# Layer 0's banded attention and six more projection columns placed between the steps of the delta rule

## The chip, the core and the metric

One program runs on one core of a Trainium2 chip. The metric is the device time of one execution in microseconds (us). The core has five engines that each take their instructions in a fixed order and wait for each other by semaphores: TensorE (PE in the profile; PEld is its weight load), VectorE (DVE), ScalarE (ACT), GpSimd (POOL) and SyncE (SP), which here issues the loads of weights. Matrix products land in eight PSUM banks of 128 x 512 floats; all other tiles lie in SBUF.

## The reference, cut to what matters

256 context tokens and 256 latent tokens of width 1024 pass through two layers, then the latent tokens through a third one. All products are in float32. The change touches the mixer of layer 0 alone:

```python
def even_mixer(u_ctx, u_lat, w_in, w_out, a_prm, sink, rope_ang, need_ctx):
    p_ctx = u_ctx @ w_in
    p_lat = u_lat @ w_in
    a_lat, a_ctx = rwkv7_mixer(p_ctx[..., :A_IN], p_lat[..., :A_IN], a_prm, need_ctx)
    qc, kc, vc = split_qkv(p_ctx[..., A_IN:], B_HEADS, B_KV_HEADS)
    ql, kl, vl = split_qkv(p_lat[..., A_IN:], B_HEADS, B_KV_HEADS)
    ...
    b_lat = banded_window_attention(ql, kl, vl, kc, vc, sink_g)
    out_lat = jnp.concatenate([a_lat, b_lat], axis=-1) @ w_out
    ...
    b_ctx = context_attention(qc, kc, vc, sink_g)
    return out_lat, jnp.concatenate([a_ctx, b_ctx], axis=-1) @ w_out
```

The first half of the mixer's output comes from a recurrence over tokens (the delta rule, `rwkv7_scan`, 8 heads of 64, in both directions, first over the context and then over the latent tokens), the second half from attention of 8 heads in which a latent query sees its band and all context keys, and a context query the context. The two halves need nothing of each other until the product with `w_out`.

## The kernel before

The modulated activations of all 512 tokens lie transposed in `uh` and `ul`, two float32r parts whose sum is the float32 value; a weight tile is split in the same way (`wchunk`: ACT writes `whi`, DVE the rest into `wlo`), and each product takes three matmuls (L259 to L261). A column of the in-projection is 128 features: 24 matmuls of 512 tokens into a bank `psT`, and a token shift by `evac_a` (one ACT, two DVE instructions). Columns 0 to 11 are r, k, v of four pairs of heads t (columns t, 4 + t, 8 + t), columns 12 to 14 the low-rank inputs; k, v and q of the attention come first, in banks of their own.

Then `b_attn` (L734) attends four heads at a time (`attn4`, L661): scores `psS` in ring `B_S` of three banks, maximum, exponential, scaling `P`, transposes `psP` in ring `B_P` of two banks, the product with v in `psO` (bank 7), and the result as two float32r parts `moB`. A builder puts each engine's instructions in their final order ahead of time; it mixes this attention with the projection of 12 columns that stands behind it in the code (L779). Columns 3, 7, 11 follow at the delta rule's third step, after which `uh`, `ul` are given up and their room becomes a pool `rwb`.

The delta rule is 16 steps n = 4 t + 2 s + d (pair of heads t, sequence s, direction d). A step has three parts. `rwkv_par` (L827) prepares decay, keys and masked products (`pw`, `pa`, `gp`, `pbk`, `pkv`, with banks from ring `B_PREP`; POOL writes `kr` and `GA`), then forms `px` and inverts a triangular matrix in five rounds inside one bank of its own, `B_INV[n % 3]`. A round is: DVE transposes `TP` and ACT copies `SP` of the last `psx`, PE `pq`, DVE `Qm`, PE `psx`. The products `pwu` and `pqm` end it, and DVE and POOL make `QM` of `pqm`. `rwkv_rec` (L989) carries the state through four chunks: PE `yp<-S,QM`, then a copy of the state by ACT and DVE, four times in turn. What a step leaves for this lies in tiles numbered y = n % NY with NY = 4, and `KX` and `QM` of a step share one of them:

```python
        KX = tl([128, 2, 2, 128], "KX", f"KQ{y}")
        ...
        QM = tl([128, 4, 128], "QM", f"KQ{y}")
```

`KX` is written from `pkv` and `px` before the inversion starts (`px` stands in the same bank as the rounds), `QM` is last read by the step's last `yp<-S,QM`. Between the steps stand 12 chunks of the modulation for later layers (`ada_chunk`, `psA`, bank 7), the gates (`gates_out`), the group norm (`rwkv_out`) and `kappa`. The last step overlaps the product with `w_out` (`pso`, `proj0`).

Of the kernel before, what the change touches and what calls it, by code (L numbers as in the profile page):

```python
# [10 lines left out]
F32 = mybir.dt.float32  # L11
# [11 lines left out]
# ---------------------------------------------------------------- constants of the shapes  # L23


def _const_tables():
    """Arrays [128, n] that depend on shapes alone."""
# [24 lines left out]
    # rope tables, features on partitions, positions 0..255 on the free axis  # L52
# [43 lines left out]
    # columns of a row of the grid; query columns run backwards inside each half, flip puts them right  # L96
# [12 lines left out]
    # retention decay, [key j, head, i - j tile offset]  # L109
# [9 lines left out]
# groups of constants that are loaded together  # L119
# [16 lines left out]
# vectors laid out with features on partitions: name -> (offset, columns)  # L136
# [16 lines left out]
def body(ctx: ExitStack, tc: tile.TileContext, A, out, dbg=None):  # L153
# [9 lines left out]
    def ring(*banks):  # L163
        """takes the PSUM banks in turn"""
# [39 lines left out]
    def rsqrt(x, scale, eps, n, name):  # L204
        """(x * scale + eps) ** -0.5 for [128, n]"""
# [16 lines left out]
    mark = {}               # last instructions of a norm, by engine  # L222
    behind, free = [], [0]  # what the parts of the weights, but for the first ones, are queued behind
# [5 lines left out]
    def wchunk(W, r0, kt, c0, n):  # L229
        """rows r0 .. r0 + 128 kt, columns c0 .. c0 + n, as a sum of two float32r parts"""  # L230
# [18 lines left out]
    def wrows(W, r0, kt, c0, n=512):  # L249
        """list over the row tiles of (hi, lo) [128, n]"""  # L250
# [48 lines left out]
    # ------------------------------------------------------------ split of an activation  # L299
# [4 lines left out]
    # ------------------------------------------------------------ adaptive modulation  # L304
# [10 lines left out]
    def ada_chunk(l, j, pool=None, bank=None):  # L315
        """columns 512 j .. of layer l"""
# [705 lines left out]
    def gates_out(t, s=None):  # L1022
# [4 lines left out]
        if gwt[t] is None:  # L1027
            gwt[t] = rw.tile([128, 512], F32, name="gw", tag="gw")
# [48 lines left out]
    n = 0  # L1077
# [728 lines left out]
```

## Time and profile before

| what | value |
|---|---|
| time, median of 3 runs | 1856.71 us (1852.91 to 1860.09) |
| the profiled execution: span from first to last instruction | 1854.7 us |
| PE, DVE, ACT, POOL busy | 1756.5, 1113.8, 960.5, 462.2 us |
| first `pw` of the delta rule, first and last `pqm` | at 189.4, 261.7 and 537.2 us |

The profile shows one execution by its span; what lies around the span is not in it, so times of runs are compared with times of runs, and the span with spans. Busy time of PE counts a matmul up to its modelled end, so matmuls that follow each other overlap in it, and the distance from one start to the next is the better price of a matmul.

### The profile page before, as it was taken

What the parts mean: (1) busy time and instruction counts of PE and PEld (TensorE: products, weight loads), DVE (VectorE), ACT (ScalarE), POOL (GpSimd) and SP (SyncE); (2) the same over time, 40 slices, a digit from 0 to 9 for tenths busy, and PEclk for the clock granted to TensorE, in tenths of its full rate; (3) what the DMA queues carried; (4) which work ended last, traced back from release to release, by engine and by line L of the source; (5) the groups of instructions that cost most, each with busy time, mean ns of one, the idle gap of its engine ahead of it and who ended that gap; (6) DMA issues with size and microseconds to landing.
All of it is one profiled execution on the core that took longest, in us unless ns stands there. A gap on an engine that the chain in (4) does not pass through costs nothing.

```text
span 1854.7 us, 31823 instructions
## 1 busy us (share of the span) xinstructions
PE 1756.5 (95%) x12273; PEld 1453.3 (78%) x12273; DVE 1113.8 (60%) x2053; ACT 960.5 (52%) x1995; POOL 462.2 (25%) x566
## 2 busy tenths in 40 slices
PE   6999989998888999999999999899989999999998
PEld 4777557665666888888888876699978879989997
DVE  3676566777746425444456457545556787558676
ACT  4554367666745454434444545455545645446554
POOL 1220444544402253333334132111120122110000
PEclk9999899999989899999999989899999999999999
DMA  9311320222136345444432320356655725655553
GB/s 313 100 51 58 115 90 14 70 70 93 46 102 220 110 136 177 149 140 139 145 114 75 102 85 13 102 159 184 192 176 177 210 75 150 185 178 175 178 182 125
DMA packets 185399, 239.93 MB, mean 129 GB/s; under 512 B 8961, under 2 KB 127889, under 8 KB 185121
## 3 DMA queue, kind: packets, MB, share of 16 engines
q1 hardware_dynamic: 183056, 229.68, 40.0%
q0 software_dynamic: 1904, 7.70, 1.3%
q8 instruction: 97, 1.59, 0.4%
q14 instruction: 54, 0.43, 0.1%
q10 hardware_dynamic: 288, 0.52, 0.1%
HBM read 236.83 MB, written 1.05 MB: 128 GB/s over the span
## 4 chain that ended last, share of the span: by engine, by line
PE 79%; DVE 7%; ACT 5%; DMA 4%; issue 2%; POOL 2%; SPq 0%; POOLq 0%; DVEq 0%; ACTq 0%
PE psT L259 11%; PE psT L260 11%; PE psT L261 11%; PE pf L264 6%; PE pf L265 6%; PE pf L266 5%; PE psU L259 2%; PE psU L261 2%; PE psU L260 2%; PE psO L723 2%; PE psS L677 2%; DMA wada<-in_w_ada_dram 2%; PE psP L713 2%; PE psN L435 1%; ACT SP L947 1%
## 5 line engine op out<-in xcount | busy, mean ns | idle before, releaser
L245 DVE TENSOR_TENSOR wlo<-raw,whi 128x1024 fp32r<-128x1024 f32 x328 | 409.1, 1254 | 296.0 <-ACT whi L244 292.8
L244 ACT ACTIVATE whi<-raw 128x1024 fp32r<-128x1024 f32 x328 | 345.5, 1056 | 290.0 <-PE psT L260 142.7
L259 PE MATMUL psT<-uh,whi 128*128 128x256 f32 (+1 forms) x1200 | 385.6, 326 | 3.1 <-ACT uh L545 0.9
L260 PE MATMUL psT<-ul,whi 128*128 128x256 f32 (+1 forms) x1200 | 384.7, 322 | 0.0
L261 PE MATMUL psT<-uh,wlo 128*128 128x256 f32 (+1 forms) x1200 | 381.8, 321 | 0.0
L259 PEld LDWEIGHTS psT<-uh,whi 128*128 128x128 f32 x1200 | 226.5, 190 | 24.5 <-issue 2.2
L260 PEld LDWEIGHTS psT<-ul,whi 128*128 128x128 f32 x1200 | 227.1, 189 | 20.9 <-issue 2.3
L261 PEld LDWEIGHTS psT<-uh,wlo 128*128 128x128 f32 x1200 | 227.0, 189 | 17.8 <-issue 0.6
L266 PE MATMUL pf<-whi,hlo 128*128 128x512 f32 x472 | 182.4, 390 | 0.0
L265 PE MATMUL pf<-wlo,hh 128*128 128x512 f32 x472 | 182.3, 390 | 0.0
L264 PE MATMUL pf<-whi,hh 128*128 128x512 f32 x472 | 181.9, 392 | 0.0
L1149 POOL TENSOR_TENSOR ffr<-ffr 128x512 f32<-128x512 f32 (+1 forms) x64 | 61.3, 958 | 288.6 <-ACT hh L1148 257.2
L266 PEld LDWEIGHTS pf<-whi,hlo 128*128 128x128 f32 x472 | 88.6, 188 | 18.8 <-issue 0.2
L265 PEld LDWEIGHTS pf<-wlo,hh 128*128 128x128 f32 x472 | 88.7, 188 | 17.6
L264 PEld LDWEIGHTS pf<-whi,hh 128*128 128x128 f32 x472 | 88.5, 188 | 17.5
L259 PE MATMUL psU<-uh,whi 128*128 128x256 f32 x352 | 98.8, 282 | 1.0 <-DVE cv L1718 1.0
L261 PE MATMUL psU<-uh,wlo 128*128 128x256 f32 x352 | 98.3, 279 | 0.0
L260 PE MATMUL psU<-ul,whi 128*128 128x256 f32 x352 | 98.3, 279 | 0.0
L353 POOL TENSOR_TENSOR adac<-adac,wadc 128x512 f32<-128x512 f32 x56 | 77.9, 1391 | 64.7 <-ACT wadc L351 47.9
L1150 DVE TENSOR_TENSOR hlo<-ffr,hh 128x512 fp32r<-128x512 f32 (+1 forms) x64 | 46.5, 727 | 74.2 <-POOL ffr L1149 74.2
L351 ACT ACTIVATE wadc<-wadc,sT 128x512 f32<-128x512 f32 x56 | 40.5, 723 | 97.2 <-DMA wadc<-in_w_ada_dram 93.8
L947 ACT ACTIVATE SP<-psx 64x128 f32<-64x128 f32 x256 | 69.4, 271 | 36.8 <-DVE TP L945 32.0
(684 smaller groups left out, 3392.7 us busy)
## 6 DMA issues: line engine op xcount, KB each, us to landing
raw<-in_w_ff_dram SPq DMA_DIRECT2D x128, 512.0 KB, 4.2
wada<-in_w_ada_dram SPq DMA_DIRECT2D x64, 512.0 KB, 4.7
raw<-in_w_in_dram SPq DMA_DIRECT2D x50, 512.0 KB, 4.4
raw<-in_w_ffn_up_dram SPq DMA_DIRECT2D x44, 512.0 KB, 4.5
wadc<-in_w_ada_dram SPq DMA_DIRECT2D x64, 256.0 KB, 2.8
raw<-in_w_out_dram SPq DMA_DIRECT2D x24, 512.0 KB, 4.8
raw<-in_w_ffn_down_dram SPq DMA_DIRECT2D x22, 512.0 KB, 4.6
raw<-in_w_in_even_dram SPq DMA_DIRECT2D x21, 512.0 KB, 5.1
```

The lines of the kernel that those rows point to most:

```text
L244: S.activation(hi[:, :tot], raw[:, :tot], AF.Copy)
L245: V.tensor_tensor(lo[:, :tot], raw[:, :tot], R(hi[:, :tot]), op=OP.subtract)
L259: T.matmul(p_, wh, xh, start=first, stop=False)
L260: T.matmul(p_, wh, xl, start=False, stop=False)
L261: T.matmul(p_, wl, xh, start=False, stop=last)
L264: T.matmul(p_, xh, wh, start=first, stop=False)
L265: T.matmul(p_, xh, wl, start=False, stop=False)
L266: T.matmul(p_, xl, wh, start=False, stop=last)
L353: G.tensor_tensor(acc, acc, w, op=OP.add)
L947: S.activation(SP[HF[c], :, e, c, :], src[HF[e], :, c, :], AF.Copy)
L1149: G.tensor_tensor(r_, r_, r_, op=OP.mult)
L1150: V.tensor_tensor(hl_, r_, R(hh), op=OP.subtract)
```

## The change

`b_attn` goes. In its place `b_pair` treats two heads of one query tile (16 calls), and the loop over the steps calls it behind steps 2 to 13: first the eight pairs of the context, then the eight of the latent tokens. Its scores have bank 2 alone, its transposes and its output bank 7 alone, which `psA`, the gates and the group norm use too; `B_PREP` is left with banks 0 and 1. `P` and `PT` lie in the weights' tiles `whi` and `wlo`, and the result replaces the queries in `qB`, so that `moB` is not needed. For the latent pairs POOL scales both halves of `P` (before: one). Six columns of the projection stand ahead of the loop, three at its second step and six at its third (before: 12, none, 3). NY is 3, and tiles that had two buffers take one in `rw` and, in odd steps, one in `rwb`.

```diff
-    B_PREP, B_INV, B_REC = ring(0, 1, 2), (ring(3), ring(4), ring(5)), ring(6)
+    B_PREP, B_INV, B_REC = ring(0, 1), (ring(3), ring(4), ring(5)), ring(6)
+    B_AS, B_AP = ring(2), ring(7)
...
-    def b_attn():
...
+    def b_pair(seq, i, t):
+        q0, nk, g = seq * 256 + i * 128, 512 if seq else 256, t // 2
+        nt, one = nk // 128, nk == 256
+        ts_ = slice(q0, q0 + 128)
...
+        P = hl[0].tile([128, 1024], F32, name="P", tag="whi")[:, :2 * nk].rearrange("p (x k) -> p x k", x=2)
+        PT = hl[0].tile([128, 1024], F32, name="PT", tag="wlo")[:, :2 * nk].rearrange("p (x k) -> p x k", x=2)
+        sk = nsink[:, 2 * t:2 * t + 2]
+        for xs in ((0, 1),) if one else ((0,), (1,)):
+            p_ = B_AS("psS")
+            for x in xs:
+                for a in range(2):
+                    T.matmul(p_[:, (x * nk if one else 0):][:, :nk], qB[:, 2 * t + x, ts_], kB[a][:, g, :nk],
+                             start=a == 0 and not (one and x), stop=a == 1, skip_group_check=one)
+            if seq:
+                m_, o = (cst["bandA"], 384) if i == 0 else (cst["bandB"], 256)
+                V.tensor_tensor(p_[:, o:o + 128], p_[:, o:o + 128], m_, op=OP.add)
+            x_ = slice(xs[0], xs[-1] + 1)
+            V.tensor_reduce(nm[:, x_], p_.rearrange("p (x k) -> p x k", x=len(xs)), axis=AX.X, op=OP.max, negate=True)
+            V.tensor_tensor(nm[:, x_], nm[:, x_], sk[:, x_], op=OP.min)
+            for x in xs:
+                S.activation(P[:, x, :], p_[:, (x * nk if one else 0):][:, :nk], AF.Exp, bias=nm[:, x:x + 1],
+                             accum_out=sums[:, x:x + 1])
...
+        V.reciprocal(sums, sums)
+        for x in range(2):
+            (V if one else G).tensor_scalar(P[:, x, :], P[:, x, :], sums[:, x:x + 1], None, op0=OP.mult)
+        for xs in ((0, 1),) if one else ((0,), (1,)):
+            tr = B_AP("psP")
+            for n_, (x, j) in enumerate((x, j) for x in xs for j in range(nt)):
+                T.transpose(tr[:, n_ * 128:(n_ + 1) * 128], P[:, x, j * 128:(j + 1) * 128], ident)
+            d_ = PT[:, xs[0]:xs[-1] + 1, :].rearrange("p x k -> p (x k)")
+            if xs[0]:
+                V.tensor_copy(d_, tr)
+            else:
+                S.activation(d_, tr, AF.Copy)
+        o_ = B_AP("psO")
+        for j in range(nt):
+            for x in range(2):
+                T.matmul(o_[x * 64:x * 64 + 64, 0:128], vBn[:, j, g * 64:g * 64 + 64], PT[:, x, j * 128:(j + 1) * 128],
+                         start=j == 0, stop=j == nt - 1)
+        S.activation(qB[:, 2 * t, ts_], o_[:, 0:128], AF.Copy)
+        V.tensor_tensor(qB[:, 2 * t + 1, ts_], o_[:, 0:128], R(qB[:, 2 * t, ts_]), op=OP.subtract)
+    b_pairs = [(seq, i, t) for seq in (0, 1) for i in range(2) for t in range(4)]
...
-    NY, NZ = 4, 3
+    NY, NZ = 3, 3
...
-    b_attn()
-    proj_a((12, 13, 14) + tuple(x * 4 + t for t in range(3) for x in range(3)))
-    cpool(cm_at, cm_attB)
+    proj_a((12, 13, 14, 0, 4, 8))
...
-    late = {x + str(y) for x in ("kr", "GA", "Gt", "KQ", "RHS", "lam") for y in (2, 3)} | {"Qm2"}
+    late = {x + "2" for x in ("kr", "GA", "Gt", "KQ", "RHS", "lam", "Qm")}
...
+        odd = rb[0] is not None and n % 2 == 1
+        def tl(shape, name, tag, bufs=1):
+            pool = rb[0] if tag in late or (bufs == 2 and odd) else rw
+            return pool.tile(shape, F32, name=name, tag=tag, bufs=1)
...
+                if n == 1:
+                    proj_a((1, 5, 9), B_LATE)
                 if n == 2:
-                    proj_a((3, 7, 11), B_LATE)
+                    proj_a((2, 6, 10, 3, 7, 11), B_LATE)
...
                 n += 1
                 for a in later[len(later) * (n - 1) // 16:len(later) * n // 16]:
                     ada_chunk(*a)
+                for a in b_pairs[16 * max(n - 3, 0) // 12:16 * max(min(n - 2, 12), 0) // 12]:
+                    b_pair(*a)
```

PE's order in the middle of the delta rule. Before, around the `px` of step 8, the rows between the steps' products are those of `psA` alone:

```order
L840 MATMUL pw<-lora,W_747 128x256
L858 MATMUL pa<-lora,A_748 128x256
L1002 MATMUL yp<-S_0_753,QM 128x128
L958 MATMUL psx<-SP_769,Qm 64x128 x4
L336 MATMUL psA_3822<-cst_ci,adar 128x128 x4
L931 MATMUL px<-RHS,GK 64x64 x8
L331 MATMUL psA<-wada,sT 32x512 x4
L1002 MATMUL yp<-S_1_754,QM 128x128
```

Now, around the `px` of step 11, scores (`psS`), transposes (`psP`) and outputs (`psO`) of latent pairs stand between the same products:

```order
L882 MATMUL pw<-lora,W_739 128x256
L784 MATMUL psO<-PT,vBn 64x128 x8
L754 MATMUL psS<-kBh,qB 128x512
L754 MATMUL psS<-kBl,qB 128x512
L1000 MATMUL psx<-SP_763,Qm 64x128 x3
L1044 MATMUL yp<-S_3_748,QM 128x128
L1000 MATMUL psx<-SP_763,Qm 64x128
L973 MATMUL px<-RHS,GK 64x64 x8
L900 MATMUL pa<-lora,A_740 128x256
L775 MATMUL psP<-cst_ci,P 128x128 x4
L993 MATMUL pq<-TP_1833,GA 64x128 x4
L1044 MATMUL yp<-S_4_749,QM 128x128
```

All of the attention but its first four scores now stands behind the first `pw`, most of it between the steps' products as here; before, all of it stood ahead of the first `pw`.

ACT's order around `KX<-pkv` of step 6. Before, it and the `KX<-px` that follows stand ahead of the first state copy of step 3 (`COPY S_5`; step 3's other two, of `S_0` and `S_1`, come 8 and 15 rows later):

```order
L919 ACTIVATE KX<-pkv 128x4x64
L947 ACTIVATE SP_2477<-psx 64x2x64 x2
L920 ACTIVATE RHS<-pkv 64x4x64
L921 ACTIVATE RHS<-pkv 64x4x64
L947 ACTIVATE SP_769<-Sx 64x2x64 x4
L947 ACTIVATE SP_2477<-psx 64x2x64 x2
L947 ACTIVATE SP_771<-psx 64x2x64 x2
L842 ACTIVATE sg<-pw,hw_1830 128x256
L947 ACTIVATE SP_771<-psx 64x2x64 x2
L850 ACTIVATE E_3862<-cs 128x256
L932 ACTIVATE KX<-px 128x4x64
L1009 COPY S_5_758<-yp 64x64
```

Now the same `KX<-pkv` of step 6 stands behind all three state copies of step 3:

```order
L1051 COPY S_5_750<-yp 64x64
L989 ACTIVATE SP_1835<-psx 64x2x64 x2
L989 ACTIVATE SP_763<-psx 64x2x64 x2
L989 ACTIVATE SP_1835<-psx 64x2x64 x2
L1051 COPY S_0_745<-yp 64x64
L950 ACTIVATE Gt<-pbk 128x4x64 x2
L1051 COPY S_1_746<-yp 64x64
L1003 ACTIVATE SP_763<-psx 64x4x64 x2
L989 ACTIVATE SP_761<-Sx 64x2x64 x4
L989 ACTIVATE SP_1835<-psx 64x2x64 x2
L961 ACTIVATE KX<-pkv 128x4x64
L962 ACTIVATE RHS<-pkv 64x4x64
```

With NY = 3, `KX` of step n lies where `QM` of step n - 3 lay, and in the new order it follows the last read of that `QM` at every step from 3 on. On SP the 13 loads of 128-column weights stand as 7, four of `wada`, 6 (before 10, four, 3), and the 40 `wada` loads behind them in one row as before.

## Rows read from the trace of the kernel before

**Rows 1.** The page, span and part 1: busy us, share, instructions.

```profile
span 1854.7 us, 31823 instructions
PE 1756.5 (95%) x12273; PEld 1453.3 (78%) x12273; DVE 1113.8 (60%) x2053; ACT 960.5 (52%) x1995; POOL 462.2 (25%) x566
```

**Rows 2.** Busy us by stretch; columns in the first row.

```profile
core 0: us, PE busy (x) PEld busy (x) DVE busy (x) ACT busy (x) POOL busy (x), PEclk, DMA share, GB/s
66.00:189.00 123.00, 119.60 (x691) 93.64 (x689) 89.16 (x220) 63.40 (x146) 18.22 (x19) 0.97 0.23 68
189.00:262.00 73.00, 63.62 (x514) 41.85 (x510) 45.66 (x102) 37.51 (x103) 31.71 (x50) 0.93 0.36 109
262.00:535.00 273.00, 244.19 (x2919) 175.94 (x2914) 194.68 (x521) 181.82 (x586) 117.30 (x188) 0.95 0.17 55
...
408.00:432.00 24.00, 21.03 (x239) 15.04 (x237) 21.65 (x55) 14.86 (x49) 13.71 (x20) 0.93 0.03 4
...
535.00:620.00 85.00, 76.03 (x381) 57.62 (x378) 51.81 (x78) 44.78 (x80) 19.39 (x27) 0.88 0.66 222
```

**Rows 3.** Waits in 262 to 535 us: us in total, times, longest.

```profile
ACT SP L947 <- DVE TP L945: 28.6, 39, 2.3
```

**Rows 4.** Timeline of PE, start us, us, instruction, count: steps 0, 3, 12 and 15.

```profile
261.72 0.61 PE L977 MATMUL pqm<-Gt,TP 128*64 128x128 f32 x8
...
268.43 0.45 PE L931 MATMUL px<-RHS,GK 128*64 128x64 f32 x6
...
278.79 0.49 PE L1002 MATMUL yp<-S,QM 128*128 128x128 f32 x2
...
322.67 0.66 PE L977 MATMUL pqm<-Gt,TP 128*64 128x128 f32 x8
...
500.57 0.69 PE L931 MATMUL px<-RHS,GK 128*64 128x64 f32 x16 [0.15 <-PE psx L958]
...
506.37 0.38 PE L1002 MATMUL yp<-S,QM 128*128 128x128 f32 x2
...
537.24 0.61 PE L977 MATMUL pqm<-Gt,TP 128*64 128x128 f32 x8
```

**Rows 5.** Timeline of PE inside attention and projection.

```profile
119.17 0.40 PE L261 MATMUL psT<-uh,wlo 128*128 128x512 f32 x1
119.40 0.39 PE L259 MATMUL psT<-uh,whi 128*128 128x512 f32 x1
...
123.06 1.09 PE L723 MATMUL psO<-PT,vBn 128*64 128x128 f32 x14
124.07 1.09 PE L713 MATMUL psP<-cst_ci,P 128*128 128x128 f32 x8
124.92 0.48 PE L677 MATMUL psS<-kBh,qB 128*128 128x512 f32 x1
```

**Rows 6.** Timeline of PE at the attention's first score.

```profile
70.24 0.39 PE L261 MATMUL psT<-uh,wlo 128*128 128x512 f32 x1
74.03 0.80 PE L677 MATMUL psS<-kBh,qB 128*128 128x512 f32 x1 [3.40 <-DVE qB L599]
...
77.61 0.63 PE L260 MATMUL psT<-ul,whi 128*128 128x512 f32 x1
78.03 0.63 PE L261 MATMUL psT<-uh,wlo 128*128 128x512 f32 x1
```

**Rows 7.** Groups by line and form, 66 to 189 us: count, busy us, mean ns.

```profile
L704 POOL TENSOR_SCALAR P<-P,sums 128x512 f32<-128x512 f32 x8 | 14.7, 1837 | 58.0 <-DVE sums L702 50.3 <-PE psP L713 7.6
L688 DVE TENSOR_REDUCE nm<-psS 128x1 f32<-128x512 f32 x16 | 10.7, 681 | 0.1
L718 DVE COPY PT<-psP 128x512 f32<-128x512 f32 x8 | 5.5, 686 | 5.2 <-PE psP L713 5.1
L702 DVE RECIPROCAL sums<-sums 128x2 f32<-128x2 f32 x16 | 2.6, 160 | 0.2
```

**Rows 8.** Timeline of PE: one chunk of the modulation in bank 7.

```profile
352.44 1.06 PE L331 MATMUL psA<-wada,sT 128*32 128x512 f32 x8
...
362.05 0.66 PE L336 MATMUL psA<-cst_ci,adar 128*128 128x128 f32 x4
```

More of the change, by code (lines that the diff above doesn't have):

```diff
@@ L463, in close_all @@
         cpool(*opened[::-1])
-    cm_mob, mob = opool("mob", side="left")
+    cm_attB, attB = opool("attB", side="left")
     cm_hl, hl[0] = opool("hl0", bufs=2, side="left")
@@ L606, in stack_k, with tmpB @@
                 V.tensor_tensor(dl[HF[x], g, :], src[HF[g]], R(dh[HF[g], g, :]), op=OP.subtract)
+    tmps = [0]
+    def tmpB(name):
+        tmps[0] += 1
+        return mix.tile([128, 512], F32, name=name, tag=("kk", "yN", "bv")[tmps[0] % 3])
     def evac_b(tag, p_):
@@ L610, in evac_b @@
         if nm == "q":
-            q_ = attB.tile([128, 512], F32, name="qB_", tag="qB_", bufs=2)
+            q_ = tmpB("qB_")
             S.activation(q_, p_, AF.Copy, scale=0.125)
@@ L615, in evac_b @@
         elif nm == "k":
-            k_ = attB.tile([128, 512], F32, name="kB_", tag="qB_", bufs=2)
+            k_ = tmpB("kB_")
             S.activation(k_, p_, AF.Copy)
@@ L657, in body @@
     cm_rc, rc = opool("rwc", side="right")
-    cm_at, at = opool("at0", side="right")
     def attn4(pool, heads, qk, vf, nk, dst_h, dst_l, sink=None, bias=None, rq=None, flip=None):
@@ L727, in attn4 @@
         V.tensor_tensor(dst_l, ov, R(dst_h), op=OP.subtract)
-    moB = [mob.tile([128, 4, 512], F32R, name=n) for n in ("moBh", "moBl")]
     nsink = cp.tile([128, 8], F32, name="nsink")
@@ L732, in body @@
     V.tensor_scalar(nsink, nsink, -1.0, None, op0=OP.mult)
[L734 to L750 removed]
+    def b_pair(seq, i, t):
+        q0, nk, g = seq * 256 + i * 128, 512 if seq else 256, t // 2
+        nt, one = nk // 128, nk == 256
+        ts_ = slice(q0, q0 + 128)
+        nm = sm.tile([128, 2], F32, name="nm", tag="nm")
+        sums = sm.tile([128, 2], F32, name="sums", tag="sums")
+        P = hl[0].tile([128, 1024], F32, name="P", tag="whi")[:, :2 * nk].rearrange("p (x k) -> p x k", x=2)
[16 more added lines that the diff above has]
+                             accum_out=sums[:, x:x + 1])
+        es = sm.tile([128, 2], F32, name="es", tag="es")
+        V.tensor_tensor(es, nm, sk, op=OP.subtract)
+        S.activation(es, es, AF.Exp)
+        V.tensor_tensor(sums, sums, es, op=OP.add)
+        V.reciprocal(sums, sums)
[17 more added lines that the diff above has]
+        V.tensor_tensor(qB[:, 2 * t + 1, ts_], o_[:, 0:128], R(qB[:, 2 * t, ts_]), op=OP.subtract)
@@ L794, in body @@
     kkt, yNt, bvt = [None] * 4, [None] * 4, [None] * 4
+    rb = [None]
     def kappa(t):
-        kk = kkt[t] = mix.tile([128, 512], F32, name=f"kk{t}", tag="kk", bufs=2)
+        own = rb[0] if t % 2 else mix
+        kk = kkt[t] = own.tile([128, 512], F32, name=f"kk{t}", tag="kk")
         S.activation(kk, pT_of(4 + t), AF.Identity, scale=vec("a_k_k", t, 1))
@@ L816, in kappa @@
         V.tensor_tensor(kk, kk, p_, op=OP.mult)
-        yNt[t] = mix.tile([128, 4, 128], F32, name=f"yN{t}", tag="yN", bufs=2)
-        bvt[t] = mix.tile([128, 512], F32, name=f"bv{t}", tag="bv", bufs=2)
-    late = {x + str(y) for x in ("kr", "GA", "Gt", "KQ", "RHS", "lam") for y in (2, 3)} | {"Qm2"}
-    rb = [None]
+        yNt[t] = own.tile([128, 4, 128], F32, name=f"yN{t}", tag="yN")
+        bvt[t] = own.tile([128, 512], F32, name=f"bv{t}", tag="bv")
+    late = {x + "2" for x in ("kr", "GA", "Gt", "KQ", "RHS", "lam", "Qm")}
     hc = CDEC * 0.5
@@ L835, in rwkv_par @@
         tk = slice(256 * s, 256 * s + 256)
-        tl = lambda shape, name, tag, bufs=1: (rb[0] if tag in late else rw).tile(shape, F32, name=name, tag=tag,
-                                                                                  bufs=bufs)
+        odd = rb[0] is not None and n % 2 == 1
+        def tl(shape, name, tag, bufs=1):
+            pool = rb[0] if tag in late or (bufs == 2 and odd) else rw
+            return pool.tile(shape, F32, name=name, tag=tag, bufs=1)
         pw = pp("pw")[:, :256]
@@ L1027, in gates_out @@
         if gwt[t] is None:
-            gwt[t] = rw.tile([128, 512], F32, name="gw", tag="gw")
+            gwt[t] = rb[0].tile([128, 512], F32, name="gw", tag="gw")
         S.activation(gwt[t][:, tk], g_, AF.Identity, scale=vec("a_gn_w", t, 1))
@@ L1044, in rwkv_out @@
         V.tensor_tensor(y3, y3, mu[:, :2 * n, None].to_broadcast([128, 2 * n, 64]), op=OP.subtract)
-        sq = rw.tile([128, 512], F32, name="sqy", tag="sq")
+        sq = rb[0].tile([128, 512], F32, name="sqy", tag="sq")
         S.activation(sq[:, tk], yf, AF.Square)
@@ L1053, in rwkv_out @@
             T.transpose(p_[:, i * 128:(i + 1) * 128], y2[:, i, :], ident)
-        o_ = rw.tile([128, 512], F32, name="ya", tag="sq")
+        o_ = rb[0].tile([128, 512], F32, name="ya", tag="sq")
         V.tensor_tensor(o_[:, tk], p_[:, :128 * n], gwt[t][:, tk], op=OP.mult)
@@ L1071, in proj0 @@
                         f = 2 * (q % 2) + k
-                        x = [(moA[f][a] if q < 2 else moB[a][:, f, :])[:, i * 128:(i + 1) * 128] for a in range(2)]
+                        x = [(moA[f][a] if q < 2 else qB[:, 2 * f + a, :])[:, i * 128:(i + 1) * 128] for a in range(2)]
                         mmX(ps0[i, ch], *x, wh[:, k, :], wl[:, k, :], q == 2 and k == 0, q == 1 and k == 1)
@@ L1109, in body @@
     cpool(cm_rb, cm_rw, cm_rc)
-    if dbg == "mix0":
-        for t in range(8):
-            m_ = moA[t][0] if t < 4 else moB[0][:, t % 4, :]
-            nc.sync.dma_start(out[0, 128 * (t % 2):128 * (t % 2) + 128, (t // 2) * 256:(t // 2) * 256 + 256],
-                              R(m_[:, 256:512]))
-        close_all()
-        return
     cm_res, res = opool("res", side="right")
@@ L1182, in body @@
         after_mix0(i, [ps0[i, 0], ps0[i, 1]])
-    cpool(cm_mix, cm_hl, cm_mob)
+    cpool(cm_mix, cm_hl, cm_attB)
     cm_hl, hl1 = opool("hl1", bufs=4, side="left")
```

17 lines of the change are left out of this document (removed).

## The prediction

> **What bounds the kernel now.** The page gives PE 1756.5 of 1854.7 us, 95% [rows 1], but that share is an average over stages with different limits, so I read the busy time by stretch next [rows 2]. From 66 to 189 us, projection and attention, PE is busy 119.6 of 123 us and every other engine has room (DVE 89.2): here the time is what PE's instructions cost, and each one taken out gives its slot back. From 189 to 262, first `pw` to first `pqm`, PE idles 9.4 of 73 us. From 262 to 535, the steps, no engine is full (PE 89%, DVE 71%, ACT 67%, POOL 43%), and PE's weight load, 64%, shows that its 89% is partly matmuls that overlap. What binds there is a loop of latencies. The list of waits shows ACT waiting for DVE's `TP` 39 times, 28.6 us together [rows 3]: an inversion round goes DVE, ACT, PE, DVE, PE, and nothing shortens it.
>
> The timeline of PE gives that loop's size [rows 4]. Three inversions run at a time, in three banks. Step 3's `px` starts at 268.4, 6.7 us after step 0's first `pqm` (261.7), in the bank that this gives up, and its own last `pqm` ends at 323.3 (322.67 + 0.66): 54.9 us for an inversion. From step 3's `px` to step 15's, 500.57, four rounds of the three banks take 232 us, 58 us each; first to last `pqm` (261.7 to 537.2) is 275.5 us or five of them. One more fact matters for the change: step 3's `px` starts **10.9 us before** step 0's last `yp<-S,QM` ends (278.79 + 0.49), step 15's 6.2 us before step 12's ends (506.37 + 0.38); the mean over the 13 steps is 9.3. Today `KX` of step n and `QM` of step n - 3 lie in different tiles, so that overlap is free.
>
> **The change part by part.**
>
> *The front.* Attention's PE instructions leave a stretch that PE bounds. Slots are distances of starts [rows 5]: 14 `psO` take 1.01 us, 0.072 each, 8 `psP` 0.85, a 512-column matmul 0.23. 192 `psO` are 13.9 us, 96 `psP` 10.2, 32 latent scores 7.5, 32 context scores at half the columns 3.9 (estimate): 35.5. By the new order 16 context scores, four transposes and four pairs of outputs stay ahead of the first `pqm`, some 3 us. **−33.** The 504 matmuls of the r/k/v projection that stand ahead of the first `pqm` stay ahead of it in both orders (432 ahead of the first `pw` and 72 behind, now 358 and 146), so moving the columns saves nothing by count.
>
> *A stall and a slow clock.* The attention's first score waits 3.40 us for `qB`, and behind it 512-column matmuls start 0.42 us apart instead of 0.23 [rows 6], which costs 14 of them some 3 us. In the new order projection stands there. −6.4 if both go, 0 if the wait finds another place; most of it is the first score's own wait, so I take **−5**.
>
> *The room from 189 to 262.* 74 more projection matmuls (17 us at 0.23) stand behind the first `pw`, where PE idles 9.4 us. Between 0 and −9.4; part of that idle time is waits for loads, which stay: **−4**. So the first `pqm` comes 42 us earlier, at about 220.
>
> *The stretch of the steps.* This is the unknown. By the rows of the two orders DVE gets 61 us more between first and last `pqm`. Of the attention [rows 7]: 24 maxima at 0.68 (16.3), 8 copies at 0.69 (5.5), 72 small ones at 0.16 (11.5), and 48 masks, context scalings and result parts at an estimated 0.3 (15); together 48, of which 4 stand earlier. Then 12 for the preparation of one more step (a whole step is 194.7 / 15 = 13), 5 for four splits of weights. DVE's work becomes 194.7 + 61 = 256 us. Nothing lengthens if DVE may fill its idle 78 us: 0. At today's 71% busy it needs 360 us, +87; at the 90% of the densest slice, 408 to 432 [rows 2], 284, +11. PE gets 33 us of matmuls on 244.2 busy, but their slots are shorter than their busy times; POOL 16 scalings of 1.84, 29 us on 117, and a `GA` or `QM` queued behind one can be late by up to 1.84.
>
> The second price is a wait. With NY = 3 `KX` of step n takes the tile that `QM` of step n - 3 had. `KX<-pkv` on ACT must now wait for that step's last `yp<-S,QM`, and `px`, which stands in the inversion's bank, is copied behind it; queued behind that copy on ACT are the `SP` of the other two inversions, for which PE's `pq` wait. In the new order it already stands behind all the state copies, so it is not the semaphore but the order that spends the time. If inversion and recurrence take as long as today, each round of the three banks grows by the overlap lost, 9.3 us, and five rounds by 47. But with `px` later there is less competition: the last inversion, which has nothing behind it, took 37.3 us (500.57 to 537.85) against 54.9. I take a quarter of the 47 back: **+36**, which is also what DVE at 83% busy would give (256 / 0.83 = 308, +35). The two prices are not added, since a longer round is itself the room in which DVE does its 61 us; ends 0 and +61 (DVE's work all in series).
>
> The Trainium skill, "Perfetto Trace Analysis", section "Optimization Strategy", advises to interleave regimes whose most-contended engine differs. The rows agree that they differ (PE in the front, latencies in the steps); by that rule alone the attention would be hidden and the sum would be that of the first rival.
>
> *The tail.* 48 of the `pso` matmuls of the product with `w_out` now stand ahead of the last `pqm`, none before; at 0.23 that is 11 us. Behind the last `pqm` PE is busy 76 of 85 us, at a granted clock of 0.88, with 222 GB/s of loads [rows 2], so not all of it comes off: 0 to −11, taken **−6**.
>
> *At nothing:* the new buffers of one in `rw` (the tiles' writers in the new order follow their readers by a whole step), the result in `qB`, `P` in the weights' tiles (no weights are split in most of that stretch), the loads on SP (7, 4, 6 in place of 10, 4, 3, hidden behind matmuls of several us each; one late one costs a wait of a few us).
>
> **Sum:** −33 − 5 − 4 + 36 − 6 = −12; 1854.7 − 12 = 1842.7. The shown median lies 2.0 above the profile's span, so **1845 us**.
>
> **The rivals.**
>
> *Hidden.* The steps' idle time takes the attention; the stretch grows by under 25 us, about 12 (DVE at 90%). For it: DVE did run at 90% in one slice, and inversions may shorten as the last one did. Against it: a DVE so full delays every `TP` and `Qm`. 1854.7 − 42 − 6 + 12 + 2 = 1821 (1811 to 1833).
>
> *The hand-over paces (slower).* Mechanism: `KX` behind the state copies, 9.3 us per round, nothing taken back, and the fuller DVE and ACT lengthen an inversion by about 5 us (a fifth more instructions to stand behind on DVE). Five rounds of 14.3 are 71: 1854.7 − 48 + 71 + 2 = 1880. It decides as soon as a round grows by more than 9.6 us (48 for five). For it: both effects lie on the loop that binds. Against it: the last inversion's 37.3. The Trainium skill, same page and section, says that a gap which keeps coming back can mean that there is too little SBUF or PSUM for the next tile; NY = 3 would make such a gap, and by that rule the change ends here. No row of before can show it.
>
> *Bank 7 paces.* `psA`, transposes, outputs and gates take turns in it. One chunk of `psA` holds it from 352.4 to 362.7, 10.3 us [rows 8]; with 12 chunks over 16 steps that is 7.7 a step, and 1.33 pairs that hold it 5 to 10 us each add 7 to 13: 14 to 21 of the 18.4 us that a step takes. At 21 the stretch grows by 15 × 2.6 = 39, about as the forecast, some 42 with the gates: 1854.7 − 48 + 42 + 2 = 1851, no change. Against it: what a pair holds is only my estimate, and context pairs are half as long.
>
> **How the numbers follow.** A change of 0.5%, 9.3 us, is about what a measurement of this kernel can tell from none. Forecast (stretch +25 to +47, 1833 to 1856): 0.43, of which 0.28 faster by more than 0.5% and 0.15 within; hidden 0.25, all faster; hand-over 0.20, of which 0.17 slower and 0.03 within; bank 7 0.12, of which 0.09 within and 0.03 slower. Faster 0.53, same 0.27, slower 0.20. The range 1815 to 1872 leaves out the lower end of hidden (0.07) and the upper part of the hand-over (0.12). The likeliest case's own range is 1833 to 1856.
>
> **What would show it.** Right: first `pqm` near 220; first to last `pqm` about 311 us, DVE about 83% busy there; every `px` from step 3 on right behind the last `yp<-S,QM` of the step three before, where it now starts ahead of it; 79 instead of 85 us from there to the tail's end. Wrong: a first `pqm` later than 230 (then the front was not PE's alone); a round of three steps over 66 us (hand-over) or under 60 (hidden); PE waiting for bank 7 rather than for DVE and ACT between the steps.

## The result and the profile after

The changed kernel takes **1875.49 us** (median of 4 runs, 1871.74 to 1881.19) against 1857.14 before: ratio 1.0111, 95% interval 1.0087 to 1.0135. It is 1.1% slower, 3.5 us above the predicted range and on the other side of no change. The profiled execution spans 1869.9 us, 15.2 more than that of before. The page's part 1, beside [rows 1]:

```profile
PE 1756.4 (94%) x12273; PEld 1448.1 (77%) x12273; DVE 1113.6 (60%) x2049; ACT 961.8 (51%) x2007; POOL 474.0 (25%) x574
```

The work is the same, so the time is a matter of where it lies. The timeline of PE (start us, us, instruction, count), beside [rows 4]:

```profile
215.67 0.61 PE L1019 MATMUL pqm<-Gt,TP 128*64 128x128 f32 x8
...
233.65 0.49 PE L1044 MATMUL yp<-S,QM 128*128 128x128 f32 x2
...
241.06 0.64 PE L973 MATMUL px<-RHS,GK 128*64 128x64 f32 x16
...
285.90 0.61 PE L1019 MATMUL pqm<-Gt,TP 128*64 128x128 f32 x8
...
522.89 1.08 PE L973 MATMUL px<-RHS,GK 128*64 128x64 f32 x16
...
568.41 0.66 PE L1019 MATMUL pqm<-Gt,TP 128*64 128x128 f32 x8
```

The first `pqm` comes 46.0 us earlier (215.7 for 261.7). First to last `pqm` takes 352.7 us for 275.5: +77.2. From the last `pqm` to the end it is 1301.5 for 1317.5: −16.0. The three make +15.2. An inversion is shorter than before (step 3's 45.5 us for 54.9), but its `px` starts late: step 3's 241.06 stands 22 us behind the end of the inversion whose bank it takes, where before it stood 3.5 behind; the mean over steps 3 to 15 is 22.2 for 4.3. A round of three steps takes 70.5 us (281.83 / 4) for 58.0.

Busy time of the engines in exactly that stretch, before and then after (columns as in [rows 2]):

```profile
261.70:537.20 275.50, 246.35 (x2968) 177.60 (x2964) 195.89 (x525) 182.99 (x588) 117.60 (x188) 0.95 0.17 55
```

```profile
215.70:568.40 352.70, 308.36 (x3424) 218.95 (x3418) 247.11 (x675) 221.51 (x700) 149.65 (x214) 0.97 0.18 59
```

There are two differences. PE is busy 62.0 us longer, and it idles 44.3 us instead of 29.2. Summed over the timeline from each matmul's start to the next one's, idle time taken out, the attention's products take 38.5 of the 62 and the `pso` that came in from the tail 12.4; the other 11 are not accounted for here. The shares of the engines have hardly moved (PE 89% to 87%, DVE 71% to 70%): before, too, PE idled only 29 us in the whole stretch.

Half of the added idle time is one wait, that of the modulation's products `psA` for their loads `wada`: 12.5 us in 8 waits, before 4.9 in 5. Whether the stretch would be shorter without it was not tried.

### The profile page after: what moved, and what is told of

It is laid out like the page before. It is cut to its first block, busy times and chain, and to the rows that moved or that the text cites. A ratio compares the mean times of both kernels' runs of the same rounds, so it can differ in the third digit from the quotient of the medians.

```text
span 1869.9 us, 31775 instructions
## 1 busy us (share of the span) xinstructions
PE 1756.4 (94%) x12273; PEld 1448.1 (77%) x12273; DVE 1113.6 (60%) x2049; ACT 961.8 (51%) x2007; POOL 474.0 (25%) x574
## 4 chain that ended last, share of the span: by engine, by line
PE 75%; DVE 7%; DMA 6%; ACT 6%; issue 2%; POOL 2%; SPq 0%; POOLq 0%; ACTq 0%; DVEq 0%
PE psT L260 10%; PE psT L261 10%; PE psT L262 9%; PE pf L265 5%; PE pf L266 5%; PE pf L267 5%; DMA wada<-in_w_ada_dram 2%; PE psU L260 2%; PE psU L262 2%; PE psU L261 2%; DMA wadc<-in_w_ada_dram 2%; PE psA L332 1%; PE pso L266 1%; PE pso L265 1%; PE psN L436 1%
## 5 line engine op out<-in xcount | busy, mean ns | idle before, releaser
L266 PEld LDWEIGHTS pf<-wlo,hh 128*128 128x128 f32 x472 | 88.6, 188 | 18.3 <-DVE wlo L246 0.8
L989 ACT ACTIVATE SP<-psx 64x128 f32<-64x128 f32 x256 | 69.2, 270 | 44.3 <-DVE TP L987 38.2
```

Source lines behind the costliest of these rows:

```text
L266: T.matmul(p_, xh, wl, start=False, stop=False)
L989: S.activation(SP[HF[c], :, e, c, :], src[HF[e], :, c, :], AF.Copy)
```

## The experiments

All ratios are to the kernel before, measured in the same job; "stretch" is first to last `pqm` in the profile, the gap is the mean from the last `pqm` of step n - 3 to the `px` of step n.

| run | us | ratio, 95% interval | stretch | gap |
|---|---|---|---|---|
| before / changed kernel | 1857.14 / 1875.49 | 1.0111 (1.0087 to 1.0135) | 275.5 / 352.7 | 4.3 / 22.2 |
| 1: before, NY = 3 | 1883.76 | 1.0167 (1.0151 to 1.0184) | 318.3 | 15.7 |
| 2: before, two preparation banks | 1896.12 | 1.0234 (1.0217 to 1.0251) | 319.0 | 18.2 |
| 3: changed, NY = 4 | 1868.47 | 1.0089 (1.0072 to 1.0107) | 341.0 | 20.5 |
| 4: changed, no attention | 1856.63 | 1.0014 (1.0000 to 1.0027) | 333.3 | 18.5 |
| 5: changed, three banks, scores in bank 7 | 1931.04 | 1.0418 (1.0392 to 1.0443) | 329.1 | 16.3 |
| 6: as 5, NY = 4 | 1923.65 | 1.0361 (1.0337 to 1.0384) | 319.8 | 12.4 |
| 7: before, NY = 3 and two banks | 1910.13 | 1.0296 (1.0261 to 1.0331) | 340.5 | 19.2 |
| 8: changed, kappa in bank 2 | 1871.61 | 1.0104 (1.0086 to 1.0122) | 345.8 | 18.3 |
| 9: as 2, kappa in bank 2 | 1874.76 | 1.0114 (1.0069 to 1.0160) | 304.0 | 7.3 |
| 10: changed, ring of three with the scores | 1872.11 | 1.0118 (1.0084 to 1.0151) | 354.8 | 22.8 |
| 11: as 10, NY = 4 | 1856.51 | 1.0019 (1.0004 to 1.0034) | 339.5 | 17.2 |
| 12: as 8, NY = 4 | 1873.98 | 1.0084 (1.0059 to 1.0110) | 347.5 | 14.2 |
| 13: as 11, no attention | 1811.68 | 0.9762 (0.9738 to 0.9787) | 280.9 | 5.6 |
| 14: changed, half of the scalings on DVE | 1870.54 | 1.0073 (1.0051 to 1.0095) | 350.3 | 21.3 |
| 15: as 13, the pairs' DVE work alone | 1838.67 | 0.9901 (0.9885 to 0.9918) | 279.8 | 4.7 |
| 16: as 11, no row maxima | 1853.89 | 0.9995 (0.9975 to 1.0016) | 340.2 | 14.3 |
| 17: before, no row maxima | 1856.19 | 0.9991 (0.9981 to 1.0002) | 278.9 | 5.4 |
| 18: as 11, the pairs without DVE work | 1846.64 | 0.9967 (0.9955 to 0.9978) | 317.2 | 12.2 |

### The two layouts, alone in the kernel before

Run 1:

```diff
-    NY, NZ = 4, 3
+    NY, NZ = 3, 3
...
-    late = {x + str(y) for x in ("kr", "GA", "Gt", "KQ", "RHS", "lam") for y in (2, 3)} | {"Qm2"}
+    late = {x + "2" for x in ("kr", "GA", "Gt", "KQ", "RHS", "lam", "Qm")}
```

> The kernel before with NY = 3 (late tiles of the set 2 alone), nothing else: attention stays ahead of the steps, three banks for the preparation. Theory H (the hand-over of all tiles named by y: kr of step n is written over a tile that the QM of step n - 3 reads, so that the preparation from kr to px, some 17 us, can't start before the inversion n - 3 has ended): every kr from step 3 on begins behind the last pqm of step n - 3, a round of three steps grows from 58 to 68 to 75 us, first to last pqm from 275 to 320 to 350, time 1895 to 1925. Theory W (the attention's own work on the fuller engines and in bank 7 is what lengthens the stretch): no growth over 10 us, time 1855 to 1867. Theory P (two preparation banks): as W.

Run 2:

```diff
-    B_PREP, B_INV, B_REC = ring(0, 1, 2), ...
+    B_PREP, B_INV, B_REC = ring(0, 1), ...
```

> The kernel before with two banks (0 and 1) for the preparation instead of three, nothing else. Theory P (with gp holding both banks, pbk and pkv wait for the masked products, and that delays every px): first to last pqm 275 grows by 30 to 60, time 1885 to 1915. Theories H and W: the preparation has slack ahead of its inversion bank (kr stood 13 to 15 us ahead of the end of the inversion three steps before), growth under 10 us, time 1855 to 1867.

Both slow the kernel by more than the whole change does, with no attention in the steps: +31 us (theory H expected more, 1895 us at the least) and +44 us. In run 1 the preparation waits for the old tile. POOL's timeline in step 3 and its waits (us in total, times, longest) from 258 to 576 us:

```profile
262.31 0.73 POOL L868 TENSOR_TENSOR kr<-kk,sg 128x256 f32<-128x256 f32 x1 [2.29 <-DVE QM L978]
```

```profile
POOL RHS L923 <- PE yp L997: 28.8, 6, 14.5
...
POOL kr L868 <- DVE QM L978: 7.8, 6, 2.3
```

`kr` of step n lies on the `kr` that `QM` of step n - 3 reads, so it starts 1.5 us behind the end of that inversion on average, where before it started 12.3 us ahead of it, and `px` needs 14 us more from there. `RHS` lies in tiles numbered y too, and its memset on POOL waits for the old one's reader `yp<-RHS,Gt` (28.8 us in 6 waits, before 4.3 in one). The step's preparation is no longer hidden under the inversion.

The hand-over that ends last is still another one. In 11 of the 13 steps the last `yp<-S,QM` of step n - 3 ends 0.3 to 5.4 us behind the `pkv` of step n, and `KX<-pkv` follows both; `px` stands 3.0 us behind that `yp<-S,QM` on average. In step 3:

```profile
270.02 0.27 PE L915 MATMUL pkv<-cst_ci,rkv 128*128 128x128 f32 x1
...
274.15 0.49 PE L1002 MATMUL yp<-S,QM 128*128 128x128 f32 x2
```

```profile
275.14 0.39 ACT L919 ACTIVATE KX<-pkv 128x256 f32<-128x256 f32 x1
```

So with NY = 3 alone the wait for `KX` that the prediction named comes last. Without it `px` could come no more than some 4 us earlier (`KX<-pkv` stands 4.1 us behind `pkv` on average): the late `kr` comes right before it.

In run 2 the tiles are as before; the preparation itself is slower, and most of all where `kappa` stands between two steps. The same place in the changed kernel, PE's timeline behind step 6:

```profile
293.31 0.27 PE L957 MATMUL pkv<-cst_ci,rkv 128*128 128x128 f32 x1
294.76 1.05 PE L843 MATMUL ssp<-cst_c,sq 128*128 128x2 f32 x8
299.30 0.60 PE L850 MATMUL psr<-cst_ci,rsn 128*2 128x128 f32 x4
302.22 1.12 PE L854 MATMUL psr<-rnT,cst_c 2*128 2x512 f32 x2
303.27 0.70 PE L882 MATMUL pw<-lora,W 64*128 64x256 f32 x2
```

and in the kernel before:

```profile
319.09 0.27 PE L915 MATMUL pkv<-cst_ci,rkv 128*128 128x128 f32 x1
...
322.04 0.70 PE L840 MATMUL pw<-lora,W 64*128 64x256 f32 x2
```

With a third bank the next step's `pw` goes ahead beside `kappa` (2.95 us from the last `pkv`); with two, `kappa`'s three products hold the banks and `pw` follows the last of them (9.96 us). Three such places make 24 us more than before in the changed kernel and 21 more in run 2. The granted clock of the stretch was 0.91 in run 2 and 0.95 before, so at most some 15 of its 44 us can be the clock's (0.09 × 319 less 0.05 × 275.5, an estimate). Run 9 takes `kappa` out of the two banks of run 2:

```diff
+    B_KAP = ring(2)
...
-        ssp = B_PREP("ssp")
+        ssp = B_KAP("ssp")
...
-        p_ = B_PREP("psr")
+        p_ = B_KAP("psr")
```

> The kernel before with two preparation banks and kappa's products in bank 2, which is empty there. Theory K: about half of the 44 us that two banks cost alone comes back, time 1868 to 1882. Rival: time 1888 to 1898.

21 of the 44 us come back, as expected: `kappa` is half of the two banks' price. Run 7 has both layouts in the kernel before:

> The kernel before with both layouts of the change, NY = 3 and two preparation banks, attention and projection ahead as before. Theory M (the two losses are two ways for the same preparation to be late, and the longer one hides the other): stretch 318 to 330, time 1892 to 1908, near the run with two banks alone. Theory A (they add): stretch 355 to 365, time 1920 to 1935.

1910 lies between the theories (stretch 340.5): the two losses hide each other in part, 44 + 31 make 56 (1910.1 against 1854.45 in that job).

### The layouts undone in the changed kernel

Run 3 gives back NY = 4, run 4 leaves the attention out:

```diff
-    NY, NZ = 3, 3
+    NY, NZ = 4, 3
...
-            pool = rb[0] if tag in late or (bufs == 2 and odd) else rw
+            pool = rb[0] if tag in late or (bufs == 2 and odd and tag in ("cs", "bk", "GK")) else rw
```

```diff
-                    b_pair(*a)
+                    pass
```

> The changed kernel with NY = 4 again (tiles of sets 2 and 3 in the pool rwb); to make room, sg, E1, ic and b_ have one place each instead of two, cs, bk and GK keep two. Theory H: kr is written well ahead of the end of the inversion n - 3 again, px follows that end by about 5 us instead of 21, first to last pqm falls from 353 to 295 to 315, time 1820 to 1840. Theories W and P: the stretch stays at 340 to 355, time 1860 to 1880.

> The changed kernel with the 16 pairs of attention left out altogether (the second half of the mixer's output is then the queries), so that NY = 3, the two preparation banks and the moved columns stand alone. Theory H: the steps stay slow, first to last pqm 325 to 345 (353 with attention), px still 15 us or more behind the end of the inversion n - 3, time 1845 to 1865. Theory W: without the attention's work the stretch falls to the 275 us of before or below, time 1795 to 1815. Theory P: as H.

Runs 5 and 6 give back the third bank and put the scores into bank 7 (6 with run 3's edit too), run 8 puts `kappa` into bank 2 (`B_PREP` to `B_AS` in its three lines, as in run 9), run 12 adds NY = 4 to that, runs 10 and 11 let preparation and scores take three banks in turn (11 with NY = 4). The edits of 5 and of 10:

```diff
-    B_PREP, B_INV, B_REC = ring(0, 1), (ring(3), ring(4), ring(5)), ring(6)
-    B_AS, B_AP = ring(2), ring(7)
+    B_PREP, B_INV, B_REC = ring(0, 1, 2), (ring(3), ring(4), ring(5)), ring(6)
+    B_AS, B_AP = ring(7), ring(7)
```

```diff
-    B_PREP, B_INV, B_REC = ring(0, 1), (ring(3), ring(4), ring(5)), ring(6)
-    B_AS, B_AP = ring(2), ring(7)
+    B_PREP, B_INV, B_REC = ring(0, 1, 2), (ring(3), ring(4), ring(5)), ring(6)
+    B_AS, B_AP = B_PREP, ring(7)
```

> The changed kernel with three banks (0, 1, 2) for the preparation again; the attention's scores go to bank 7, to its transposes and outputs. NY stays 3. Theory P (in the changed kernel the serial preparation in two banks binds, 23.7 us from one pw to the next, and NY = 3 hides behind it): the preparation becomes faster until NY = 3 binds, as in the run of before with NY = 3 (62.6 us per three steps): stretch 353 falls to 325 to 340, time 1848 to 1865. Theory B7 (bank 7 is then the bound: scores, transposes, outputs, psA, gates in one bank): stretch 353 or longer, time 1872 to 1900.

> Both layouts of before in the changed kernel: three preparation banks (scores in bank 7) and NY = 4 (sg, E1, ic, b_ with one place). If the two layouts are all that lengthens the stretch beyond the attention's own 19 us: stretch 275 + 19 to 35 = 295 to 310, time 1810 to 1832, faster than both kernels. If bank 7 paces: stretch 340 or more, time 1860 and up.

> The changed kernel, with the three products of kappa (ssp, psr, psr) put into bank 2, where the attention's scores are, instead of the two preparation banks. Theory K (with two banks kappa, which stands between steps 2 and 3, 6 and 7, 10 and 11, holds the serial preparation: from pkv of those steps to the next pw 10 to 12 us, where before had 3): these three distances fall to 3 to 5 us, stretch 353 to 325 to 340, time 1850 to 1865. Rival (the two banks cost the same at every step, gp, pbk and pkv waiting for each other): the distances may fall but px does not come earlier, time 1868 to 1880.

> The changed kernel with banks 0, 1 and 2 in one ring of three that the preparation and the attention's scores take in turn, bank 7 as in the change; NY = 3. If a third bank for the preparation is what is missing and sharing it with the scores costs little: NY = 3 binds then, stretch 325 to 340, time 1845 to 1862. If a score in the ring holds the preparation as kappa does: stretch 345 and more, time 1868 to 1890.

> The same with NY = 4 (sg, E1, ic and b_ with one place): both layouts of before, bank 7 without the scores. If the two layouts are what the change loses: stretch 295 to 320, time 1815 to 1840, faster than before. If scores in the ring hold the preparation: stretch 335 and more, time 1858 to 1885.

> The changed kernel with two preparation banks, kappa's products in bank 2 with the scores, and NY = 4 (sg, E1, ic and b_ with one place). With kappa out of the two banks the kr stood right behind the end of the inversion three steps before (NY = 3 bound then). If these two are the layout's losses: stretch 346 falls to 310 to 328, time 1832 to 1850. If the attention's own work in the steps binds once they are gone (as in the ring of three with NY = 4): stretch 335 to 345, time 1855 to 1866.

Theory H, that NY = 3 is the whole cause, falls with run 3, which gains 4 to 7 us (by the ratios and by the medians). Run 4 came out as H and P said. Run 8 removes the three gaps at `kappa` (0.6 to 3.3 us from `pkv` to `pw`) and gains at most 4 us, with `kr` 3.0 us behind the inversion's end: NY = 3 takes over. Run 12 removes that too (`kr` 5.2 us ahead of it on average), and the stretch is still 347, above both expectations. Run 10 shortens nothing (stretch 354.8), as if a score in the ring held the preparation like `kappa`, which is not shown. Run 11, with the layouts of before, is level with before at 1856.5, not faster. Runs 5 and 6 show the rival of bank 7 where scores share it: their steps are shorter (329 and 320), but behind the last `pqm` of run 6 48 `psO` and 60 `psA` are left over, and PE is busy only half the time there:

```profile
533.00:573.00 40.00, 20.60 (x127) 11.86 (x126) 11.06 (x34) 6.26 (x18) 7.03 (x5) 0.59 0.16 53
```

In the changed kernel itself nothing of the pairs is left over behind the last `pqm`.

### What the attention costs in the steps

Run 13 takes the attention out of run 11, run 14 gives DVE one half of the scalings back:

```diff
-            (V if one else G).tensor_scalar(P[:, x, :], ...
+            (G if x and not one else V).tensor_scalar(P[:, x, :], ...
```

> The ring of three banks with NY = 4, and the 16 pairs of attention left out (second half of the mixer's output is the queries): the steps as in before but for the moved projection columns and single places. Theory O (the losses overlap: either late preparation or the attention's own work holds a step, so that taking one away shows little): the stretch falls to 275 to 292, that is, in a good layout the attention costs 50 us and more of stretch where it cost 20 in the change's, time 1795 to 1815. Theory R (something else that the change brought, moved columns or the shared places, lengthens the steps): stretch 310 to 335, time 1830 to 1850.

> The changed kernel with one half of each latent P scaled on DVE, as before the change, instead of both on GpSimd: 8 scalings of 1.84 us leave GpSimd, 8 of 0.69 come to DVE. If scalings on GpSimd hold sums, GA or QM on the path: faster by 5 to 12 us, 1863 to 1870. If DVE and the layout decide: no change, 1870 to 1880.

Without attention the undone layout takes 1811.7 us and a stretch of 280.9, so the attention costs 45 us there (1856.5 − 1811.7) and only 19 in the changed kernel (1875.5 − 1856.6), whose preparation is late anyway. That 19 is a lower bound, because run 4 got less clock in the stretch (0.88 for 0.97). That the losses overlap is seen without run 4: the two layouts cost 56 us with the attention in the front (run 7) and 19 with it in the steps (1875.5 − 1856.5, run 11), and that is why undoing one of them showed little. Run 14 gains 5 us by the medians and 7 by the ratios, between its two expectations: the second half on GpSimd is a small part of the loss.

Which engine the 45 us are paid on: run 15 keeps only the pairs' VectorE instructions, run 16 drops the row maxima (the shift cancels in the softmax), run 17 does that in the kernel before, run 18 keeps all but the VectorE instructions. The edits of 15 and 18 are those that their expectations name. Run 16 is the following, with the small instructions on `nm` and `es` gone too; run 17 does the same in `attn4`.

```diff
-            V.tensor_reduce(nm[:, x_], ..., op=OP.max, negate=True)
-            V.tensor_tensor(nm[:, x_], nm[:, x_], sk[:, x_], op=OP.min)
...
-                S.activation(P[:, x, :], ..., AF.Exp, bias=nm[:, x:x + 1], ...)
+                S.activation(P[:, x, :], ..., AF.Exp, bias=sk[:, x:x + 1], ...)
```

> The ring of three banks with NY = 4, and of each attention pair the VectorE instructions alone, with the same operations and sizes (masks, maxima, small ones, reciprocals, scalings of the context, copies and subtractions of the latent), read from the queries in SBUF and written to the tiles of P and PT, whose values nobody uses: no scores, exponentials, transposes, products, no bank. The second half of the mixer's output is the queries. Without attention this layout took 1812 us with a stretch of 281, with it 1857 and 340. Theory D (VectorE's work in the steps is the price): stretch 318 to 340, time 1838 to 1857. Theory S (the banks, and the pairs' chains of PE, ScalarE and GpSimd, are the price): stretch 281 to 300, time 1812 to 1826.

> The ring of three banks with NY = 4 and the whole attention, but without the row maxima: the exponential subtracts the sink alone (the shift cancels in the softmax), so that 24 maxima of 0.68 us and 40 small VectorE instructions go, some 22 us of VectorE, 1 us of ScalarE, and a score leaves its bank a maximum earlier. Theory D: stretch 340 falls by 22 to 35, time 1825 to 1838, faster than before. Theory S: only the scores' hold is shorter, stretch falls by under 12, time 1846 to 1857.

> The kernel before with the same removal of the row maxima in layer 0's attention, which stands there in the front, where PE bounds: no change by either theory (1850 to 1858); faster by over 8 us only if the front hangs on VectorE after all.

> The ring of three banks with NY = 4 and every matmul, transpose, bank and GpSimd instruction of the attention pairs in place, but none of their VectorE instructions: no masks, no maxima, no sums, no scaling of the context, the second copy of the transposes on ScalarE, the result's second part left out (the attention's values are then not the reference's). With all of it 1857 us and a stretch of 340, without attention 1812 and 281. Theory D (VectorE's 48 us are the price): stretch 281 to 300, time 1812 to 1826. Theory T (TensorE's own order is the price: some 33 us of slots and the waits of the pairs' products in a queue that is 88 to 90% busy in all these runs): stretch 320 to 340, time 1838 to 1856.

Run 15 did not put its work where it was meant to: its instructions hang on nothing, were ordered ahead of the first `pqm` (240.7 instead of 217.5) and left the stretch at 279.8. It shows only that 27 us are lost when VectorE gets this work in the steps' beginning. Run 17 came out as expected, no change. Run 16 takes 16 us of VectorE's busy time out of the stretch (251.3 to 235.0), and the stretch stays (340.2): VectorE alone is not it. Run 18 decides more. The stretch (columns as in [rows 2]) without attention (run 13), without the VectorE part (run 18), and with all of it (run 11):

```profile
217.50:498.40 280.90, 252.21 (x3008) 178.09 (x3009) 203.35 (x540) 187.92 (x597) 119.21 (x189) 0.98 0.20 64
```

```profile
211.50:528.70 317.20, 290.21 (x3388) 206.72 (x3383) 209.93 (x545) 223.67 (x701) 143.67 (x204) 0.99 0.20 64
```

```profile
217.70:557.20 339.50, 301.44 (x3436) 216.51 (x3432) 251.30 (x687) 223.48 (x708) 143.14 (x204) 0.97 0.20 65
```

From 13 to 18 the stretch grows by 36.3 us, PE's busy time by 38.0, its idle time not at all (28.7 to 27.0). From 18 to 11 it grows by 22.3, of which idle time is 11.1. So the larger part, 35 of 45 us (1846.6 − 1811.7), stays when VectorE is spared, and shows as busy time of PE: the products' own slots are 39 to 40 us by the timeline in these runs, in a queue that idled under 30. That these slots alone are the price is argued, not shown. Run 18 also keeps ScalarE's 36 and GpSimd's 24 us, and its scores share the ring of the preparation's banks; from 13 to 18 the inversions keep their length (52.2 and 52.7 us on average, steps 3 to 14) and the gap ahead of `px` grows by 6.6 us, so it is the preparation that comes later. A run with the scores in a bank that nothing else uses, beside three banks for the preparation, was not made.

## Why the prediction was wrong

**The front** was right: −46.0 for −42, first `pqm` at 215.7 for 220, first `pw` at 129.9.

**The stretch** failed: +77 for +36, and beyond the bound of +61. Three steps of the argument did.

First, "no engine is full" and "what binds there is a loop of latencies". The row said 244.2 of 273 us for PE, and I let the weight load's 64% talk it down to matmuls that overlap. The windows' busy time counts a moment once, so what is left of it is idle time: 29 us, in waits of at most 2.0 us. That is a lower bound of what is free, since a matmul counts as busy up to its modelled end (eight `pqm` last 0.61 us, and the next products start 0.44 us behind the first of them). Even so the attention's slots, 36 us in the front and 38.5 here, were priced at nothing in the stretch: the sum's price there was DVE's work and one wait. DVE's work came as summed (247 us for 256), but at 70% busy and not at the 83% forecast. Run 13 against 11 is the measure of the missing term: 45 us in the steps for the 46 that the front gained; 35 of the 45 remain with VectorE spared (run 18).

The Trainium skill, "Perfetto Trace Analysis", section "Identifying the Most-Contended Engine", would judge TensorE's headroom by MFU and the weight load's busy share, not by matmul busy time. By that measure there was room here: the weight load stood at 63 to 65% of the stretch in runs 13, 18 and 11 alike. The stretch grew all the same, from 281 to 317 and 340 us, and matmul busy time (90, 91, 89%) was the share that left little. By busy time PE was the fullest engine in the front (97%) and in the steps (89%), so "the rows agree that they differ" was a misreading, and the advice to interleave did not apply.

Second, the third preparation bank was given up at no cost: `B_PREP` stands in no term of my sum. Alone it costs 44 us, half of it by `kappa`.

Third, the hand-over of the tiles. For NY = 3 alone the sign was right, and the wait for `KX` does come last there, but it is not the only one: `kr` and `RHS` go through the same hand-over a few us before. That the size agrees (run 1: stretch +43 for 36 to 47) is partly luck. A round of three steps grew by 4.6 us only (62.6 for 58.0), because the inversions became 5 us shorter (48.1 for 53.2); the rest is a first `px` that stands 11 us later behind the first `pqm` and a last inversion that is 13 us longer. In the changed kernel the wait named is no longer what holds `px`. My sign was "every `px` from step 3 on right behind the last `yp<-S,QM`"; it starts 10.3 us later than that on average, and only in 3 of 13 steps (6, 10 and 14) does that `yp<-S,QM` end behind the step's own `pkv`. In the other ten the preparation is later still.

The Trainium skill's sentence on consistent bubbles (same page, "Optimization Strategy") fits runs 1 and 2. With one buffer less the gap ahead of `px` came back every step, 15.7 and 18.2 us on average for 4.3, and PE's idle time in the stretch rose from 29 to 52 and 47 us.

These prices don't add. Less the `pso` matmuls that came into it from the tail (72, 34 and 48 at 0.23 us), the stretch grew by 48 us through the two layouts (run 7), by 51 through the attention in a good layout (run 11 against 13), and by 66 through both together. The likely reason is that a step that waits for its preparation has room for the attention.

**The tail** was too small, −16 for −6, and the larger part of it came from elsewhere. The 48 `pso` matmuls went ahead as forecast (12.4 us of their slots are paid again in the stretch), but from the last `pqm` to the end of the last `pso` it takes 60.1 us for 61.6: 37 `psN` of the next block came in their place, and PE idles 9.5 us there for 4.8. The other −14.5 lie behind the last `pso`, where no term of the sum looked. Before, PE stands 2.74 us ahead of `psSh` there, and its 256-column matmuls then start 0.21 us apart up to 619 us; after, both `psSh` come 20 us before the last `pso`, and the next block's products follow at once, 0.12 apart. From the end of the last `pso` on, the kernel before and its five variants take 1250 to 1256 us and the changed one with its variants 1237 to 1244. The windows of the two places, before and after, at a granted clock of 0.73 and 1.00:

```profile
598.00:630.00 32.00, 28.20 (x143) 22.93 (x142) 21.68 (x33) 15.61 (x31) 11.20 (x12) 0.73 0.55 178
```

```profile
628.00:650.00 22.00, 20.27 (x153) 18.30 (x152) 15.61 (x19) 13.49 (x23) 4.84 (x6) 1.00 0.74 240
```

**The rivals.** The slower one, "the hand-over paces", gave 1880 and came nearest; its round of three steps was to exceed 66 us, and it measured 70.5, by other means than its inversions, which became shorter. "Hidden" fell. Bank 7 shows little in the changed kernel (PE's waits for its earlier users, `psP` behind `adas` and `psA` and `pg` behind `ya`, make 3.3 of the 44 us of idle time), and holds work back in runs 5 and 6. No version with the whole attention was faster than before beyond its interval; run 16 is level (0.9975 to 1.0016).

## What to carry to other kernels

Before work is moved into another stage, take that stage's idle time on the same engine (length of the stretch less busy time in the windows) and set the moved slots against it; here an idle 10% in crumbs of 2 us took little. A buffer or a bank that is given up to make room has a price of its own, worked out by what is written into it next and how long ahead of its turn that was ready before (here `kr`, 12 us). Losses through late preparation and through added work hide each other, so undo them together, and once without the moved work, before concluding that none of them matters.

## What the hardware showed unexpectedly

Leaving the attention out of the changed kernel (run 4) lowered the granted clock of the stretch:

```profile
217.40:550.70 333.30, 288.27 (x3086) 208.09 (x3081) 215.32 (x547) 192.03 (x607) 123.23 (x198) 0.88 0.19 61
```

PE was idle 45 of 333 us there and 0.88 was granted, a mean over stretches at 2.4 and at 1.2 GHz; run 13, idle 29 of 281, got 0.98. The sum of idle time alone does not tell the clock: the changed kernel idled 44 of 353 us and got 0.97. So run 4's 1857 us hold a loss by the clock too, and its 19 us for the attention are a lower bound. Taken at its most, the loss is some 29 us (0.12 × 333.3 less 0.03 × 352.7, an estimate), so run 4 does not tell how much less than 45 us the attention costs in the changed kernel.
